# Turning band probabilities in 32x32 squares on VectorE, and band values as 32x64 tiles, in a hybrid decoder layer

## The chip, the cores and the metric

The kernel runs on one core of a Trainium2 chip. The core has five engines, each with its own instruction queue that it takes in order: TensorE (PE in the profile, with its weight loads as PEld), VectorE (DVE), ScalarE (ACT), GpSimd (POOL) and SyncE (SP), which here only issues DMAs; GpSimd issues DMAs too. Data lie in SBUF (128 partitions) and in PSUM (8 banks of 128 x 512 f32), which TensorE writes and VectorE and ScalarE read.

The metric is the device time of one execution in microseconds, lower is better. Before the change it is 1550.65 us, the median of 3 runs (1550.27 to 1556.05).

## The reference, cut to what matters

One layer over 4096 new prompt tokens (width 1024) and 64 sample tokens. After an RMS norm one projection makes the columns of three head groups: a gated short convolution, banded attention, and cross-attention into 256 memory tokens. The groups are gated, concatenated and sent through an output projection with a norm and a residual. The change concerns the banded attention of the prompt:

```python
# q (B, S, 2, 4, 64); k, v (B, S, 2, 64); blocks of 128 queries, 256 keys (previous block and own block)
qb = q.reshape(b, nb, 128, 2, 4, 64)
kk = concat([previous k block, k block]); vv = the same of v
diff = a + 128 - j                       # a: query 0..127, j: key 0..255
mask = (diff >= 0) & (diff < 128) & key exists
s = einsum('...qkgd,...skd->...kgqs', qb, kk) * 64 ** -0.5
m = max(max(where(mask, s, -inf)), sink) # one learned sink logit a head
p = exp(s - m) / (sum(exp(s - m)) + exp(sink - m))
o = einsum('...kgqs,...skd->...qkgd', p, vv)
out_b = silu(gate) * o                   # then cross-attention beside it, and the output projection
```

Every query sees exactly 128 keys: keys 0..a of its own block and keys a+1..127 of the block before. All is f32.

## The kernel before, in words

The work has two parts. The **input projection** (0 to about 950 us, products at line 359) makes all projected columns in three phases of blocks of 520 tokens and writes them to DRAM: queries and keys as pairs of a rounded value and its remainder (`qd`), V (`vd`, transposed: 128 columns of head dimension by tokens) and the gates (`md`). During its third phase `third_jobs` puts small jobs between the products: the memory keys and values, and the attention of the first 256 prompt tokens ("early").

The **attention stage** (about 950 us to the end) runs 33 blocks in order, `Block.run`: 0 to 30, 32 (the sample tokens), 31. A block is 128 output rows: two halves of 512 columns, each 24 products of 128x512 (line 1471: `y<-wo,mh` and `y<-wo,ml`, the gated mix split into a rounded part `mh` and a remainder `ml`, lines 1447 and 1450). Between these products `events_of` hangs the attention of later query groups. A group is 128 queries; a chunk is two groups (256 tokens). Names in the trace:

- `ws`: band scores, 24 products with 64 rows a tile; `xs`: 12 cross scores. ScalarE copies the own-block half into `sm` (L1140), and VectorE overwrites it with the previous-block half where the mask says so (L1141): the 128 keys that a query sees, folded into one 128x128 square a head, so `sm` is 128 x (8 heads x 128 keys).
- `band_softmax`: VectorE's maximum (`wmx`, L1147), ScalarE's eight exponentials (L1152), `wden`, `wrd` (L1153, L1154), and VectorE's product `sm` x `wrd` (L1155). `cross_softmax` does the like on `xp`, with GpSimd's scaling (L1167).
- `transposes`: eight 128x128 transposes of `sm` on TensorE (`wt`, L1194), eight of `xp` (`xt`, L1207), copies to `pt` and `xpt` by ScalarE (L1195) and VectorE or ScalarE (L1208). GpSimd's two selects take the folded square apart: `wpv` keeps the previous block's keys (L1199), `wpt` the own block's (L1201).
- `values` (`pv`): cross values in 128x64 tiles, band values in 128x64 and 64x64 tiles on V transposed by TensorE (`vtp`, L1075), into a two-bank tile; then two gates on VectorE (L1219, L1254) multiply into `mix`.

In block i: `values_and_scores` at the start of the first half makes the scores of group i+3, then the values of group i+1, then the softmax of group i+3. `transposes` at the start of the second half turns group i+2. `split` of block i+1 makes `mh` and `ml` from `mix` later in that half. At the end of each half VectorE multiplies y by the norm weights (`yn`, L1478) and ScalarE squares it (L1479); after the second half come `yst`, GpSimd's power (L1485) and the residual (`xr`, L1489).

The order on an engine is made by a scheduler from the program, except where `keep_in_program_order` holds an instruction in its place. Loads are on SP's queue (`vT`, `mix`, `xr`) and on GpSimd's (`kst`, `q`).

Of the kernel before, what the change touches and what calls it, by code (L numbers as in the profile page):

```python
# [15 lines left out]
P = 128  # L16
# [35 lines left out]
def hybrid_layer(ctx: ExitStack, tc: tile.TileContext, a: dict):  # L52
# [28 lines left out]
    vd = tc.dram_tile([P, NT], F32, name="vd")  # L81
    md = tc.dram_tile([KT, P, NT], F32, name="md")
# [711 lines left out]
    def third_jobs(b, p):  # L794
# [19 lines left out]
        if n > 13 and third["chunk"]:  # L814
            jobs.append(third["chunk"].pop(0))
        elif n > 13 and len(chunks) == 1:
            jobs.append(lambda: (chunk_load(1), chunks[1].load_values()))
# [7 lines left out]
    early = [0]  # L825

    def first_chunk():
# [5 lines left out]
        chunk.load_values()  # L833
        chunk.load_mix()
        third["chunk"] = [lambda: chunk.values(None)]
# [66 lines left out]
    def input_projection():  # L902
        for i, (ph, b, p) in enumerate(steps):
# [36 lines left out]
            if ph == 2 and b == last:  # L940
                for j in ((), (), (0, 1, 2), (3, 4, 5), (6, 7), (8, 9, 10, 11), (12, 13, 14, 15))[p]:
                    jobs.append(lambda j=j: wo_split(j))
                for j in ((), (0, 2, 4), (), (6, 8), (10, 12), (14,), ())[p]:
                    jobs.append(lambda j=j: wo_load(j))
                if p == 6:
                    jobs.append(blocks[0].split)
# [35 lines left out]
    def open_attention():  # L982
# [6 lines left out]
        ps = {tag: ctx.enter_context(tc.tile_pool(name=f"ps{tag}", bufs=1, space=bass.MemoryType.PSUM)) for tag in ("pv", "b")}  # L989
        vp = ctx.enter_context(tc.tile_pool(name="vp", bufs=5, side="right"))  # L990
# [9 lines left out]
    def psum(bank, name):  # L1000
# [3 lines left out]
        return ps["b"].tile([P, 512], F32, tag=f"b{bank}", name=name)  # L1004

    def values_psum(name):
        return ps["pv"].tile([P, 2, 512], F32, tag="pv", name=name)
# [5 lines left out]
    run_open = [False]  # L1013

    def tiled(o, w, x, **kw):

        ins = TE.matmul(o, w, x, **kw)  # L1017
        if run_open[0] and ps is not None:
            tc.keep_in_program_order(ins)
        run_open[0] = True  # L1020
# [10 lines left out]
    class Chunk:  # L1031
# [38 lines left out]
        def values(self, vt_prev, pv=None):  # L1070

            self.vts = [vt_prev]
            ts = [psum(0, f"vtp{self.c}_{i}")[:, 0:P] if pv is None else pv[:, P * i : P * i + P] for i in range(2)]
            for i in range(2):
                TE.transpose(ts[i], self.vT[:, i * P : i * P + P], ident)  # L1075
            for i in range(2):
                if self.c == 0:
                    vt = third["vt"] if i else third["work"].tile([P, P], F32, tag="v", name="vt0_0", bufs=1)
                else:
                    vt = vp.tile([P, P], F32, tag="v", name=f"vt{self.c}_{i}")  # L1080
                S.mul(vt, ts[i], 0.5)
                self.vts.append(vt)

    class Group:
# [6 lines left out]
        def open_scores(self, n):  # L1091
            b = self.b
            if n == 0:
                t = wp.tile([P, D], F32, tag="sm", name=f"sm{b}", bufs=1) if b % 2 and b > 1 else work(f"sm{b}")
                self.sm = t.rearrange("p (h k) -> p h k", h=8)
            if n == 3:
                t = wp.tile([P, D], F32, tag="p", name=f"xp{b}", bufs=1) if b % 2 and b > 1 else work(f"xp{b}")
# [45 lines left out]
        def band_softmax(self):  # L1143
# [11 lines left out]
            V.tensor_tensor(sm, sm, rd.unsqueeze(2).to_broadcast([P, n, P]), op=ALU.mult)  # L1155
# [47 lines left out]
        def cross_transposes(self, u, t):  # L1203
            t3 = t.rearrange("p (k n) -> p k n", k=2)
            for kt in range(2):
                for j in range(2):
                    TE.transpose(t3[:, kt, j * P : (j + 1) * P], self.p[:, u, j, kt * P : (kt + 1) * P], ident)  # L1207
            (S.copy if u else V.tensor_copy)(self.xpt[u], t)  # L1208
# [25 lines left out]
        def values(self):  # L1234

            c, pv = self.chunk, values_psum(f"pv{self.b}")
            self.cross_values(pv[:, 0, 256 : 256 + CT])
            o = pv[:, :, :256].rearrange("p a (h q) -> p a h q", h=4)
            step = lambda n, kvh: (c.vts[self.i + n], (self.pv, self.pt)[n][kvh].rearrange("p (h q) -> p h q", h=4))
            for n in range(2):  # L1240
                for kvh in range(2):
                    cs = slice(64 * kvh, 64 * kvh + 64)
                    v, p3 = step(n, kvh)
                    tiled(o[cs, n], v[:, cs], p3[:, :, 64 * n : 64 * n + 64], start=True, stop=False,
                          tile_position=(0, 64 * kvh))
            for n in range(2):
                for kvh in range(2):
                    cs, rs = slice(64 * kvh, 64 * kvh + 64), slice(64 - 64 * n, 128 - 64 * n)
                    v, p3 = step(n, kvh)
                    tiled(o[cs, 1 - n], v[rs, cs], p3[rs, :, 64 - 64 * n : 128 - 64 * n], start=False, stop=True,  # L1250
                          tile_position=(64 - 64 * n, 64 * kvh))
            self.cross_gate(pv[:, 0, 256 : 256 + CT])
            g = c.mix[:, 4:8, self.i * P : self.i * P + P].rearrange("p h (a q) -> p a h q", a=2)
            V.tensor_tensor(g, g, o, op=ALU.mult)  # L1254
# [3 lines left out]
    def values_and_scores(i):  # L1258

        run_open[0] = i == 0  # L1260
        g = i + 3
        if g < 2 * NCH:
            groups[g] = Group(chunks[g // 2], g % 2)
            groups[g].scores()
        if 2 <= i + 1 < 2 * NCH:
            groups.pop(i + 1).values()
        if g < 2 * NCH:
            groups[g].band_softmax()

    def transposes(i):  # L1270
        g, c = i + 2, (i + 2) // 2
        if g < 2 * NCH:
            if g % 2 == 0:
                chunks[c].values(chunks[c - 1].vts[2], psum(0, "vtp1")[:, :CT] if c == 1 else values_psum(f"vtp{c}")[:, 1, 256:])
            groups[g].transposes()
# [17 lines left out]
    def sample_mem(bh):  # L1293
# [18 lines left out]
        s = psum(3, f"sms{bh}")[:, :256]  # L1312
# [11 lines left out]
        transpose_to(pt, [(p[:, kt * P : (kt + 1) * P], P) for kt in range(2)], 3, f"smt{bh}")  # L1324
        pt = pt.rearrange("p (a c) -> p a c", a=2)
        yield
        o = values_psum(f"smo{bh}")[:, 0, :256]
# [7 lines left out]
        t = psum(3, f"smot{bh}")  # L1335
# [12 lines left out]
    def sample_window():  # L1348
# [20 lines left out]
        vn = vp.tile([P, P], F32, tag="v", name="svn")[:64]  # L1369
        transpose_to(vn, [(zs[:, 5, :], 64)], 1, "svnt")  # L1370
# [3 lines left out]
        for half in range(2):  # L1374
            s = psum(1 + half, f"sws{half}")
# [26 lines left out]
        pt, ptn = work("swpt").rearrange("p (a n) -> p a n", a=2)[:, 0], work("swptn")[:64, :512]  # L1402
        transpose_to(pt, [(sm[i][:, 0:P], P) for i in range(4)], 1, "swt0")
        transpose_to(ptn, [(sm[i][:, P:192], 64) for i in range(4)], 2, "swt1")
        pt = pt.rearrange("p (a b) -> p a b", a=4)
        yield
        o = values_psum("swo")[:, 0]
        o3 = o.rearrange("p (b c) -> p b c", b=NB)
        TE.matmul(o, vn, ptn, start=True, stop=False)
# [14 lines left out]
    class Block:  # L1424
# [28 lines left out]
        def run(self, last, events):  # L1453
# [6 lines left out]
            for p, (c0, c1) in enumerate(parts):  # L1460
                if b == 0:
                    both = values_psum("y0") if p == 0 else both
                    acc = both[:, p]
                else:
                    acc = psum((0, 5, 1)[p], f"y{b}_{p}")[:, : c1 - c0]
                j, passes = 0, 3 if m == P else 2
                for k in range(KT):
                    for fn in events.get((min(p, 1), k), ()) if p < 2 else ():
                        fn()
                    for l, r in ((0, 0), (1, 0), (0, 1)) if m == P else ((0, 0), (0, 1)):  # L1470
                        TE.matmul(acc, self.hl[l][:, k], wo[k][c0 // 512][:, r, c0 % 512 : c0 % 512 + c1 - c0], start=j == 0, stop=j == passes * KT - 1)  # L1471
# [7 lines left out]
                S.activation((psum(2, "sq") if end else acc)[:m, : c1 - c0], acc[:m], AF.Square, scale=float(D) ** -0.5, accum_out=st[:m, p : p + 1])  # L1479
# [8 lines left out]
            for cs in (slice(0, 512), slice(512, D)) if last else (slice(0, D),):  # L1488
# [6 lines left out]
    open_attention()  # L1495
    chunks[1].load_mix()
    chunk_load(2)
    chunks[2].load_values()
# [6 lines left out]
    sample = {(26, 1, 4): mem0, (27, 0, 5): mem0, (27, 1, 4): mem0, (27, 1, 6): mem0, (28, 0, 5): mem0,  # L1505
              (28, 1, 4): mem1, (29, 0, 5): mem1, (29, 1, 4): mem1, (29, 1, 6): mem1, (30, 0, 5): mem1,
              (28, 1, 5): window, (29, 0, 4): window, (29, 1, 5): window, (30, 0, 4): window}

    def events_of(i):
# [9 lines left out]
        if i % 2 == 0:  # L1519
            at(0, 1 if i else 4, chunk_load, i // 2 + 3)  # L1520
            if i // 2 + 3 < NCH:
                at(1, 3, lambda: chunks[i // 2 + 3].load_values())
            if i == 28:
                at(0, 1, lambda: chunks[15].load_mix())
        elif (i + 3) // 2 < NCH - 1:
# [123 lines left out]
```

## Time and profile before

| | |
|---|---|
| median of 3 runs | 1550.65 us |
| the profiled execution | 1549.02 us, of which the span is 1547.3 |
| granted TensorE clock in it | 0.997 of full speed |
| PE busy | 1525.7 us (99%) |
| DVE busy | 1124.6 us (73%) |
| ACT busy | 776.8 us (50%) |
| POOL busy | 335.6 us (22%) |
| DMA | 299.47 MB, q1 46.1% and q0 16.9% of 16 engines' time |

A row of a timeline gives the start in us from the span's start, the length in us, the engine, the line of the kernel, the operation, output <- inputs, and how many were merged. In brackets stands the idle time of the engine just before, and what ended it. A row of the groups gives busy time in all, the mean of one in ns, and the idle time ahead with its releasers. Lengths of matmuls overlap, since they are pipelined, so the spacing of starts tells their cost. A row of the chain of waits gives the start, the length and the engine and line that the end of the span was waiting for at that time.

### The profile page before, as it was taken

The numbers are of one execution on the slowest core, as the hardware profiler recorded it, in microseconds if no ns is written. First come the engines' busy times: TensorE is split into PE (matmuls) and PEld (weight loads), VectorE is DVE, ScalarE is ACT, GpSimd is POOL, SyncE is SP. The second block draws the span as 40 slices with busy tenths as digits, with TensorE's granted clock in tenths as the row PEclk, the third lists the DMA queues.
The fourth block names the chain that finished last, engine by engine and source line by source line (L and its number), as shares of the span: only waits on it lengthen the run. The fifth ranks groups of instructions, "written<-read, shape, count | busy, mean of one in ns | idle before, by whom it ended". The sixth has DMA issues, their size and how long they took to land.

```text
span 1547.3 us, 30906 instructions
## 1 busy us (share of the span) xinstructions
PE 1525.7 (99%) x11981; PEld 1400.8 (91%) x11981; DVE 1124.6 (73%) x1850; ACT 776.8 (50%) x1964; POOL 335.6 (22%) x522
## 2 busy tenths in 40 slices
PE   9999999999999999999999998999999999999998
PEld 9999999999999999999999997788888888888776
DVE  6779888897988777996776678566666666666654
ACT  6776566475222222344454445555555555555541
POOL 0323323220400000000000101343333434334320
PEclk9999999999999999999999999999999999999999
DMA  9979999877755333669666859744554544445432
GB/s 260 212 204 257 262 274 266 276 243 269 198 179 179 125 125 126 215 209 304 234 216 199 255 189 299 219 145 137 143 161 147 150 137 137 137 137 160 153 107 96
DMA packets 169735, 299.47 MB, mean 194 GB/s; under 512 B 29813, under 2 KB 99445, under 8 KB 169557
## 3 DMA queue, kind: packets, MB, share of 16 engines
q1 hardware_dynamic: 128069, 226.69, 46.1%
q0 software_dynamic: 40800, 69.76, 16.9%
q8 instruction: 94, 1.54, 0.4%
q10 hardware_dynamic: 720, 1.05, 0.2%
q14 instruction: 52, 0.43, 0.1%
HBM read 190.38 MB, written 108.05 MB: 193 GB/s over the span
## 4 chain that ended last, share of the span: by engine, by line
PE 88%; DVE 4%; issue 3%; DMA 2%; ACT 2%; POOL 1%; SPq 0%; DVEq 0%; POOLq 0%; ACTq 0%
PE c L359 49%; PE y L1471 24%; PE pv L1017 5%; PE ws L1017 3%; PE xt L1207 2%; PE xs L1017 2%; PE wt L1194 2%; PE mem_acc L775 1%; DMA wor<-in_w_out 1%; ACT sm L1152 1%; DMA vd<-v 1%; DVE z L366 0%; DMA wr_2A<-in_w_in 0%; DVE wo L182 0%; POOL md L163 0%
## 5 line engine op out<-in xcount | busy, mean ns | idle before, releaser
L1471 PE MATMUL y<-wo,mh 128*128 128x512 f32 (+1 forms) x1040 | 338.6, 396 | 4.6 <-ACT y L1479 3.3
L366 DVE TENSOR_TENSOR z<-c,z 128x520 f32<-128x520 f32 (+1 forms) x308 | 194.7, 645 | 96.8 <-PE c L359 95.7
L1471 PEld LDWEIGHTS y<-wo,mh 128*128 128x128 f32 x1040 | 195.5, 189 | 56.3 <-DVE sm L1141 10.8
L1471 PE MATMUL y<-wo,ml 128*128 128x512 f32 (+1 forms) x520 | 202.5, 390 | 2.7 <-DVE ml L1450 2.7
L1471 PEld LDWEIGHTS y<-wo,ml 128*128 128x128 f32 x520 | 98.5, 189 | 20.8 <-DVE ml L1450 3.0
L1163 ACT ACTIVATE xp<-xs,xnm 128x256 f32<-128x256 f32 x128 | 59.5, 471 | 115.0 <-DVE xnm L1161 101.8
L1479 ACT ACTIVATE y<-y 128x512 f32<-128x512 f32 (+1 forms) x66 | 38.2, 578 | 130.8 <-DVE yn L1478 130.8
L1167 POOL TENSOR_SCALAR xp<-xp,xrd 128x256 f32<-128x256 f32 x128 | 61.5, 491 | 181.8 <-DVE xnm L1161 111.9
L1152 ACT ACTIVATE sm<-sm,wnm 128x128 f32<-128x128 f32 x256 | 99.1, 388 | 3.0 <-DVE wnm L1148 3.0
L1199 POOL TENSOR_SCALAR_AFFINE_SELECT wpv<-wpt 128x512 f32<-128x512 f32 x62 | 62.4, 1018 | 115.5 <-ACT wpt L1195 109.8
L1153 DVE TENSOR_TENSOR wden<-wden,wes 128x8 f32<-128x8 f32 x32 | 5.3, 167 | 88.3 <-ACT sm L1152 88.3
L1478 DVE TENSOR_TENSOR yn<-y,gpost 128x512 f32<-128x512 f32 (+1 forms) x66 | 45.1, 684 | 27.1 <-PE y L1471 26.4
L1017 PEld LDWEIGHTS ws<-kst,q 64*128 64x128 f32 x768 | 48.3, 188 | 11.3 <-issue 10.5
L734 POOL MEMSET negs<- 128x1 f32 x1 | 0.1, 98 | 264.4 <-PE c L359 264.4
L1017 PE MATMUL ws<-kst,q 64*128 64x256 f32 x768 | 55.4, 290 | 0.0
L368 ACT COPY z<-c 128x520 f32<-128x520 f32 (+1 forms) x44 | 24.4, 554 | 55.5 <-PE c L359 52.9
L1201 POOL TENSOR_SCALAR_AFFINE_SELECT wpt<-wpt 128x512 f32<-128x512 f32 x64 | 40.3, 639 | 52.7 <-ACT wpt L1195 50.5
L1141 DVE COPY_PREDICATED sm<-wmask,ws 128x256 f32<-128x256 uint8 x124 | 48.0, 441 | 4.5 <-ACT sm L1140 3.2
L1485 POOL TENSOR_TENSOR yst<-yst,mhalf 128x1 f32<-128x1 f32 (+1 forms) x33 | 18.4, 557 | 151.0 <-DVE yst L1484 151.0
L1489 DVE SCALAR_TENSOR_TENSOR xr<-yn,yst,xr 128x1024 f32<-128x1024 f32 (+2 forms) x34 | 42.5, 1253 | 8.1 <-POOL yst L1485 8.1
L400 ACT CAST zh<-z 128x520 fp32r<-128x520 f32 x56 | 33.4, 624 | 29.7 <-DVE z L366 26.9
L1152 ACT ACTIVATION_READ_ACCUMULATOR sm<-sm,wnm 128x1 f32 x256 | 48.2, 188 | 0.0
(957 smaller groups left out, 5064.1 us busy)
## 6 DMA issues: line engine op xcount, KB each, us to landing
q<-qd POOLq DMA_DIRECT2D x32, 768.0 KB, 8.5
xr<-in_x_p SPq DMA_DIRECT2D x32, 512.0 KB
nat<-in_x_p SPq DMA_DIRECT2D x39, 416.0 KB
o_yp<-xr SPq DMA_DIRECT2D x31, 512.0 KB
md<-th POOLq DMA_DIRECT2D x48, 260.0 KB, 6.6
qd<-zh SPq DMA_DIRECT2D x48, 260.0 KB
qd<-z SPq DMA_DIRECT2D x48, 260.0 KB
place<-md SPq DMA_DIRECT2D x8, 1024.0 KB
```

Of the source, the lines that this page charges most:

```text
L359: TE.matmul(bank[:, :HW], l, r, start=first and i == 0, stop=last and i == 3 * KH - 1)
L366: add = lambda dst, other: V.tensor_tensor(dst, c, other, op=ALU.add)
L1017: ins = TE.matmul(o, w, x, **kw)
L1141: V.copy_predicated(to, third["wmask"], third["negs"].unsqueeze(2).to_broadcast([P, 2, P]) if self.b == 0 else s3[:, :, 0:P])
L1152: S.activation(sm[:, h, :], sm[:, h, :], AF.Exp, bias=nm[:, h : h + 1], scale=SCALE, accum_out=den[:, h : h + 1])
L1163: S.activation(p[:, i, :], s[:, i, :], AF.Exp, bias=nm[:, i : i + 1], scale=SCALE, accum_out=den[:, i : i + 1])
L1167: G.tensor_scalar(p[:, i, :], p[:, i, :], rd[:, i : i + 1], 0.5, op0=ALU.mult, op1=ALU.mult)
L1199: G.affine_select(self.pv[u].rearrange("p (h q) -> p h q", h=4), p3, pattern=[[0, 4], [-1, P]], compare_op=ALU.is_gt, fill=0.0, base=0, ch ...
L1201: G.affine_select(p3, p3, pattern=[[0, 4], [1, P]], compare_op=ALU.is_ge, fill=0.0, base=0, channel_multiplier=-1)
L1471: TE.matmul(acc, self.hl[l][:, k], wo[k][c0 // 512][:, r, c0 % 512 : c0 % 512 + c1 - c0], start=j == 0, stop=j == passes * KT - 1)
L1478: V.tensor_tensor(yn[:m, c0:c1], acc[:m], gpost[:m, c0:c1], op=ALU.mult)
L1489: V.scalar_tensor_tensor(self.xr[:m, cs], yn[:m, cs], st[:m, 3:4], self.xr[:m, cs], op0=ALU.mult, op1=ALU.add)
```

## The change

- **Turning the probabilities.** `transposes` keeps only the cross part (both copies now ScalarE's). A new `turn` takes the normalised square `sm` apart first, with two GpSimd selects of 128x1024 (`sp` for the previous block, `sm` in place for the own block), and then turns each by one VectorE transpose, which transposes every 32x32 square in its place: `t1` and `t0`, 128x1024 each.
- **Normalising.** VectorE's product `sm` x `wrd` becomes eight GpSimd scalings of 128x128, with the factor 0.5 of the gate.
- **Values.** After turns in squares, key 32k+r of query 32g+c stands in partition 32g+r. So the rows g of the array take queries 32g to 32g+31, and V must stand in all four groups of 32 partitions. Five steps (the five squares of 32 keys that a group of 32 queries touches), four row groups, two kv heads: 40 products of 32x64 tiles with 128 columns, into four PSUM banks, then four gates of 128x128.
- **V.** In the third phase, `v_load` and `v_turn` read `vd` in eight parts of 512 tokens, turn them in squares on VectorE and write them by four DMAs each to DRAM as `vn` (tokens by head dimension). `load_values` reads a chunk of it four times, once for each group of 32 partitions. TensorE's transposes of V go, except in the first chunk.
- **Order and places.** In block i: scores and softmax of group i+2 at the start of the first half; values of group i+1 at the start of the second half; `split` after its fourth step, cross transposes of group i+2 after its fifth, `turn` after its sixth. y has two banks of its own (6, 7); scores and band values share banks 0 to 3, cross scores and cross transposes banks 4 and 5. Mix and V are loaded in odd blocks. The sample stages move to other places. Transposes, the first y product and those after an event are held in program order.

```diff
+    vn = tc.dram_tile([NT - NS, P], F32, name="vn")
...
+        if n >= 15 and n % 3 == 0 and n < 39:
+            jobs.append(lambda: v_load((n - 15) // 3))
+        if n >= 17 and n % 3 == 2 and n < 41:
+            jobs.append(lambda: v_turn((n - 17) // 3))
...
+    def v_turn(k):
+        turned = temp(f"vq{k}")[:, :512]
+        V.transpose(turned, third.pop(("v", k)))
+        rows_of = vn[512 * k : 512 * k + 512, :].rearrange("(b i) d -> i b d", i=32)
+        for g in range(4):
+            ds = slice(32 * g, 32 * g + 32)
+            DMA.dma_start(rows_of[:, :, ds], turned[ds].rearrange("p (b j) -> p b j", j=32))
...
-            self.vT = self.pool().tile([P, CT], F32, tag="vT", name=f"vT{self.c}")
-            DMA.dma_start(self.vT, vd[:, self.ts])
+            self.vr = vp.tile([P, 8, P], F32, tag="vr", name=f"vr{self.c}")
+            for g in range(4):
+                DMA.dma_start(self.vr[32 * g : 32 * g + 32], vn[CT * self.c : CT * self.c + CT, :].rearrange("(b i) d -> i b d", i=32))
...
-            V.tensor_tensor(sm, sm, rd.unsqueeze(2).to_broadcast([P, n, P]), op=ALU.mult)
+            for h in range(n):
+                G.tensor_scalar(sm[:, h], sm[:, h], rd[:, h : h + 1], 0.5, op0=ALU.mult, op1=ALU.mult)
...
+        def turn(self):
+            flat = lambda t: t.rearrange("p h k -> p (h k)")
+            parts = self.sm, wp.tile([P, 8, P], F32, tag="sp", name=f"sp{self.b}", bufs=1)
+            G.affine_select(parts[1], self.sm, pattern=[[0, 8], [1, P]], compare_op=ALU.is_gt, fill=0.0, base=0, channel_multiplier=-1)
+            G.affine_select(parts[0], self.sm, pattern=[[0, 8], [-1, P]], compare_op=ALU.is_ge, fill=0.0, base=0, channel_multiplier=1)
+            self.turned = [wp.tile([P, 8, P], F32, tag=f"t{n}", name=f"t{n}_{self.b}", bufs=1) for n in range(2)]
+            for n in (1, 0):
+                tc.keep_in_program_order(V.transpose(flat(self.turned[n]), flat(parts[n])))
...
         def transposes(self):
             for u in range(2):
-                self.pt[u], self.pv[u] = (wp.tile([P, 512], F32, tag=t, name=f"w{t}{self.b}_{u}") for t in ("pt", "pv"))
-                self.band_transposes(u, psum(1 + u, f"wt{self.b}_{u}"))
-            for u in range(2):
                 self.xpt[u] = wp.tile([P, 512], F32, tag="xpt", name=f"xpt{self.b}_{u}")
-                self.cross_transposes(u, psum(3 + u, f"xt{self.b}_{u}"))
+                self.cross_transposes(u, psum(4 + u, f"xt{self.b}_{u}"))
...
-            (S.copy if u else V.tensor_copy)(self.xpt[u], t)
+            S.copy(self.xpt[u], t)
...
+            outs = [psum(g, f"wo{self.b}_{g}") for g in range(4)]
+            cross = outs[3][:, P : P + CT]
+            self.cross_values(cross)
+            for step in range(5):
+                for g in range(4):
+                    for kvh in range(2):
+                        rs, cs = slice(32 * g, 32 * g + 32), slice(64 * kvh, 64 * kvh + 64)
+                        now, k = (0, step) if step <= g else (1, step - 1)
+                        v = c.vr[rs, 4 * self.i + k, cs] if now == 0 else (last.vr[rs, 4 + k, cs] if self.i == 0 else c.vr[rs, k, cs])
+                        tiled(outs[g][cs, :P], v, self.turned[now][rs, 4 * kvh : 4 * kvh + 4, 32 * k : 32 * k + 32],
+                              start=step == 0, stop=step == 4, tile_position=(32 * g, 64 * kvh))
+            self.cross_gate(cross)
+            for g in range(4):
+                t = self.i * P + 32 * g
+                gate = c.mix[:, 4:8, t : t + 32]
+                V.tensor_tensor(gate, gate, outs[g][:, :P].rearrange("p (h q) -> p h q", h=4), op=ALU.mult)
...
-        at(0, 0 if i else 3, values_and_scores, i)
+        at(0, 0, scores, i + 2)
...
-        at(1, 0 if i else 2, transposes, i)
+        at(1, 0, values, i + 1)
         if i + 1 < len(blocks) and blocks[i + 1].b != 32:
-            at(1, 3 if i else 4, blocks[i + 1].split)
+            at(1, 4, blocks[i + 1].split)
+        at(1, 5, after_scores, i + 2, Group.transposes)
+        at(1, 6, after_scores, i + 2, Group.turn)
```

More of the change, by code (lines that the diff above doesn't have):

```diff
@@ L1068, in load_mix, with early_values @@
             DMA.dma_start(self.mix, md[:, :, self.ts].rearrange("k p n -> p k n"))
[L1070 to L1073 removed]
+        def early_values(self):
+            vT = self.pool().tile([P, CT], F32, tag="vT", name="vT0")
+            DMA.dma_start(vT, vd[:, self.ts])
+            ts = [psum(0, f"vtp{i}")[:, 0:P] for i in range(2)]
             for i in range(2):
[L1075 removed]
+                TE.transpose(ts[i], vT[:, i * P : i * P + P], ident)
+            self.vts = [None]
             for i in range(2):
[L1077 to L1081, printed above, removed]
+                vt = third["vt"] if i else third["work"].tile([P, P], F32, tag="v", name="vt0", bufs=1)
+                S.copy(vt, ts[i])
                 self.vts.append(vt)
@@ L1270, in transposes, with values, after_scores @@
[L1270 to L1275, printed above, removed]
+            groups[g].band_softmax()
+    def values(g):
+        if 2 <= g < 2 * NCH:
+            groups.pop(g).values()
+    def after_scores(g, fn):
+        if g < 2 * NCH:
+            fn(groups[g])
     def chunk_load(c):
@@ L1495, in hybrid_layer @@
     open_attention()
+    chunk_load(2)
+    for c in range(2):
+        chunks[c].load_values()
     chunks[1].load_mix()
-    chunk_load(2)
-    chunks[2].load_values()
     blocks[0].load()
```

124 lines of the change are left out of this document (50 added, 74 removed).

## The prediction

> **What bounds the kernel now.** I read the page first, then the chain that ended last, then the timelines of PE, DVE, ACT and POOL over one block of the attention stage (about 950 us to the end; one block makes 128 output rows).
>
> ```profile
> PE 1525.7 (99%) x11981; PEld 1400.8 (91%) x11981; DVE 1124.6 (73%) x1850; ACT 776.8 (50%) x1964; POOL 335.6 (22%) x522
> PE 88%; DVE 4%; issue 3%; DMA 2%; ACT 2%; POOL 1%; SPq 0%; DVEq 0%; POOLq 0%; ACTq 0%
> L366 DVE TENSOR_TENSOR z<-c,z 128x520 f32<-128x520 f32 (+1 forms) x308 | 194.7, 645 | 96.8 <-PE c L359 95.7
> ```
>
> TensorE is busy 99% of the span and is 88% of the chain. In the input projection VectorE waits for it (95.7 us ahead of L366). In the attention stage the chain shows the scores (`ws`) at the same place of every second block:
>
> ```profile
> 1137.43 1.62 PE ws L1017 x23
> 1173.46 1.62 PE ws L1017 x23
> ```
>
> Two blocks take 36.03 us, so a block takes 18.02. Its PE work, from PE's timeline:
>
> ```profile
> 1139.89 1.09 PE L1017 MATMUL pv<-xpt,mv 128*64 128x128 f32 x16
> 1140.81 0.60 PE L1017 MATMUL pv<-wpv,vt 128*64 128x256 f32 x4
> 1141.78 0.43 PE L1017 MATMUL pv<-wpv,vt 64*64 64x256 f32 x2
> 1141.79 0.43 PE L1017 MATMUL pv<-wpt,vt 64*64 64x256 f32 x2
> 1142.04 0.38 PE L1017 MATMUL pv<-wpv,vt 64*64 64x256 f32 x2
> 1142.37 0.50 PE L1471 MATMUL y<-wo,mh 128*128 128x512 f32 x1
> 1147.96 0.38 PE L1075 MATMUL vtp<-ident,vT 128*128 128x128 f32 x2
> 1148.18 1.04 PE L1194 MATMUL wt<-ident,sm 128*128 128x128 f32 x8
> 1149.05 1.04 PE L1207 MATMUL xt<-ident,xp 128*128 128x128 f32 x8
> ```
>
> **TensorE's share of the change.** Removed: the eight band transposes, 1149.05 - 1148.18 = 0.87 us a block, and the two of V, 0.22 us a chunk (0.11 a block). The band values take 1142.37 - 1140.81 = 1.56 us now. They become 40 products on eight 32x64 tiles; this trace records an f32 product as two instructions, so 80, in ten rounds of eight tiles and 128 columns. In the 64*64 part four tiles start within 0.01 us and the next round 0.26 us later for 256 columns; the cross values make eight rounds of 128 columns in 0.92 us, 0.115 each. A round then costs 0.115 to about 0.15: 1.15 to 1.5 us in all. If the 32-row tiles did not run side by side and each instruction took what one takes in the cross values (0.92/16 = 0.0575), it would be 4.6 us. I take 1.5, by the 64*64 rows, the nearest form. PE's block: 18.02 - 0.87 - 0.11 - 0.06 = 16.98 us, with ends 16.6 and 20.1. If PE stayed the bound, this would save about 1 us a block.
>
> **What the change puts in VectorE's way.** One block of the other engines, from their timelines (DVE, then ACT, then POOL):
>
> ```profile
> 1137.46 0.69 DVE L1478 TENSOR_TENSOR yn<-y,gpost 128x512 f32<-128x512 f32 x1 [0.47 <-PE y L1471]
> 1139.23 0.45 DVE L1141 COPY_PREDICATED sm<-wmask,ws 128x256 f32<-128x256 uint8 x1
> 1139.85 1.28 DVE L1489 SCALAR_TENSOR_TENSOR xr<-yn,yst,xr 128x1024 f32<-128x1024 f32 x1 [0.17 <-POOL yst L1485]
> 1143.31 1.21 DVE L1147 TENSOR_REDUCE wmx<-sm 128x8 f32<-128x1024 f32 x1
> 1144.76 0.41 DVE L1219 TENSOR_TENSOR mix<-mix,pv 128x256 f32<-128x256 f32 x1
> 1145.09 0.68 DVE L1254 TENSOR_TENSOR mix<-mix,pv 128x512 f32<-128x512 f32 x1
> 1149.33 0.20 DVE L1154 RECIPROCAL wrd<-wden 128x8 f32<-128x8 f32 x1
> 1149.57 1.22 DVE L1155 TENSOR_TENSOR sm<-sm,wrd 128x1024 f32<-128x1024 f32 x1
> 1150.71 0.68 DVE L1478 TENSOR_TENSOR yn<-y,gpost 128x512 f32<-128x512 f32 x1
> 1151.31 0.68 DVE L1208 COPY xpt<-xt 128x512 f32<-128x512 f32 x1
> 1154.12 1.23 DVE L1450 TENSOR_TENSOR ml<-mix,mh 128x1024 fp32r<-128x1024 f32 x1 [2.13 <-ACT mh L1447]
> ```
> ```profile
> 1145.79 0.39 ACT L1152 ACTIVATE sm<-sm,wnm 128x128 f32<-128x128 f32 x1
> 1148.91 0.19 ACT L1152 ACTIVATION_READ_ACCUMULATOR sm<-sm,wnm 128x1 f32 x1
> 1153.01 1.07 ACT L1447 CAST mh<-mix 128x1024 fp32r<-128x1024 f32 x1
> ```
> ```profile
> 1144.82 0.93 POOL L1167 TENSOR_SCALAR xp<-xp,xrd 128x256 f32<-128x256 f32 x2 [2.60 <-DVE xnm L1161]
> 1146.18 0.93 POOL L1167 TENSOR_SCALAR xp<-xp,xrd 128x256 f32<-128x256 f32 x2 [0.44 <-DVE wes L1149]
> 1149.96 1.33 POOL L1199 TENSOR_SCALAR_AFFINE_SELECT wpv<-wpt 128x512 f32<-128x512 f32 x1 [2.84 <-ACT wpt L1195]
> 1151.35 0.64 POOL L1201 TENSOR_SCALAR_AFFINE_SELECT wpt<-wpt 128x512 f32<-128x512 f32 x1
> masks.py:199 POOL TENSOR_SCALAR_AFFINE_SELECT ident<-ident 128x128 f32<-128x128 f32 x1 | 0.3, 284 | 0.0
> ```
>
> In the changed program, as built, VectorE's order in each block is: `yn` of the second half of block i; the four masked copies, maxima and small operations of group i+3; `yn` of the first half of block i+1; `wden` and `wrd` of group i+3; the five gates of group i+2 and `ml`; the two turns of group i+3; then `yn` of the second half of block i+1. An engine takes its queue in order, so nothing of group i+4 can start on VectorE before both turns of group i+3 are done, and these wait for GpSimd, which waits for `wrd`. The softmax of one group thus becomes a closed loop over VectorE, ScalarE and GpSimd. The old loop was shorter: from `yn` at 1137.46 through the softmax to the `yn` behind it at 1150.71, 13.25 us, well inside 18.02.
>
> The new loop, counted from that `yn`:
> - `yn`, ScalarE's square, the masked copies, the maxima and the eight exponentials up to the end of `wrd`: 1149.53 - 1137.46 = 12.07 us. The order inside is nearly the same, and its last member is the exponentials (1145.79 to 1149.10). GpSimd then starts about 0.09 us later, as `xp` at 1146.18 does behind its reciprocal: 12.16.
> - Eight scalings of 128x128 on GpSimd replace the one VectorE product of 1.22 us. The nearest row, 128x256, takes 0.465; selects grow from 0.284 us (128x128) to 0.64 (128x512), 0.93 ns an element, so half the width saves about 0.12: 0.35 each, 2.8 us. Ends: 0.23 (half of 0.465) and 0.465, 1.9 and 3.7 us. At 14.96.
> - Two selects of 128x1024: 0.64 + 512 x 0.93 ns = 1.11 us each and two gaps of 0.06: 17.3. Upper end two 128x512 each, 1.28.
> - GpSimd held up by VectorE: `wpv` at 1149.96 took 1.33 us, not 0.64, while the product at 1149.57 with two SBUF operands ran beside it, though the pair of `xp` scalings took 0.93 beside the gates, which read PSUM, as without them. `ml` has two SBUF operands. It is due inside this leg: gates from 12.1 to 13.3 (four of 128x128: 0.41 at 256 and 0.68 at 512 columns make 0.28, less 0.08 of overlap; one at 0.33; the old pair took 1.01), `mh` 1.07 and `ml` 1.23 to about 15.7. In the old row 0.69 us were lost of 0.83 beside the product; over all of `ml` that is 1.0. At 18.3. Ends: 0 and 1.25.
> - The turns: `t1` runs beside the second select; `t0` follows it. No row shows a 32x32 turn on VectorE. The nearest by size and type are the 128x1024 operations at 1.21 and 1.22 us; I take 1.22 and subtract the 0.08 by which successors overlap. The ends are 0.68 (the 128x512 copy) and 2.44, twice as long. L = 19.5 us.
>
> [...]
>
> So L = 19.5 is longer than PE's 16.98, and VectorE's loop sets the pace; PE would idle 2.5 us a block. Other edits cost nothing while this holds: the gates and `mh`/`ml` lie beside GpSimd's leg; `xpt` goes to ScalarE, which loses two `wpt` copies for it; scores and values share banks 0 to 3, but scores of group i+4 need only the gates of group i+2 (at 13.3), before PE's y needs `ml` at 15.7.
>
> V: eight loads, eight turns of 128x512 (0.68 each by the copy) and 32 stores lie in the input projection, under VectorE's waits for PE (L366). On SP's queue each store waits for its turn, and behind it stand the projection's loads; those are issued three products ahead, some 13 us. Cost 0, upper end 8 x 0.68 = 5 us. Four reloads a chunk, with one, go out two blocks early; cost 0.
>
> **Start and end.**
>
> ```profile
> 953.32 0.50 PE L1471 MATMUL y<-wo,ml 128*128 128x512 f32 x1 [2.73 <-DVE ml L1450]
> 975.36 0.69 DVE L1478 TENSOR_TENSOR yn<-y,gpost 128x512 f32<-128x512 f32 x1 [2.84 <-PE y L1471]
> 1483.44 0.69 DVE L1478 TENSOR_TENSOR yn<-y,gpost 128x512 f32<-128x512 f32 x1 [0.39 <-PE y L1471]
> 1505.50 1.09 PE L1017 MATMUL pv<-xpt,mv 128*64 128x128 f32 x16
> ```
> ```profile
> L1387 DVE COPY_PREDICATED_SCALAR ssm<-smask,negs 128x384 f32 x2 | 1.3, 656 | 3.7 <-ACT ssm L1384 3.7
> L1400 DVE TENSOR_SCALAR ssm<-ssm,swrd 128x192 f32<-128x192 f32 x4 | 1.0, 316 | 0.0
> ```
>
> Block 0 now holds no scores, and its split is issued earlier: y from about 951, 48 products at 0.233 (24 of them lie between 1142.37 and 1147.96, 5.59 us) and eight transposes later `yn` of its second half comes at 963 (end 966), not 975.4. From there 28 loops lead to block 28's `yn` (now 1483.4). Behind it, group 31: `ml` at 15.7, some 8 us of sample work that stands before the turns (the six operations of the last two rows, 2.6 us, and an estimate of 5 to 6 for some ten more, four of them exponentials), the turns 2.4: 26. Its values take 2.5. What follows took 1547.3 - 1505.5 - 2.5 = 39.3, less the 5.6 of the half block that now lies ahead: 33.7. Together 62.2 against 63.9.
>
> Span = 963 + 28 x 19.5 + 62.2 = 1571.2; with the profiled run's 1.7 us around the span (1549.02 against 1547.3), **1573 us**, against 1549.0 of that execution, itself 1.6 under the median of 1550.65. In short: time = 1027 + 28 L. Equal at L = 18.64. About 0.5% (7.75 us) is what a measurement here can tell: faster below 18.37, slower above 18.92.
>
> **Rivals.**
> 1. *Faster: GpSimd's leg is short.* If `ml` does not hold it and the scalings cost 0.3, the leg from `wrd` to the end of the selects is 4.7 us, not 6.2: L = 18.05, time 1532. It decides at a leg of about 5.05 us. Held scalings elsewhere (1.33 against 0.64) speak against; that part of `ml` may fall before the selects speaks for. The floor is PE's block: 16.98, 1502.
> 2. *The turns take 2.44 us each:* `t1` then ends behind the second select, L about 22, time 1643. No row decides this.
> 3. *PE is the bound after all,* with the values at 4.6 us: L = 20.1, time 1590. Against: four 64*64 tiles start together.
> [...]
>
> **Chances.** Loop between 18.9 and 20.5, the forecast: 0.49, slower. Loop 18.4 to 18.9: 0.10, same. Rival 1: 0.24, faster. Rival 2: 0.09, rival 3: 0.08, both slower. So slower 0.66. The forecast's own range is 1556 to 1601. The range over all leaves out the far ends of rivals 1 and 2: 1526 to 1622.
>
> **What would show it.** Right: in the changed kernel VectorE's turn waits for GpSimd's select, the chain of waits in this stage runs through exponentials, scalings, selects and turns, PE idles about 2.5 us a block, and blocks are 19.5 us apart. Wrong: PE stays near 99% and blocks are 17 us apart (rival 1), or a turn row shows over 2 us, or the values' group spans over 3 us. A clock row below 1.00 in PE's new gaps would add time that no term here holds.

## The result and the profile after

The changed kernel takes 1602.79 us (median of 4 runs, 1601.2 to 1605.24), the kernel before 1550.46 (median of 4): ratio 1.033, 95% interval 1.0303 to 1.0358. It is slower by 52 us, where the prediction had it slower by 24. The profiled execution has a span of 1600.1 us against 1547.3.

The page, its busy times and the chain that ended last by engine:

```profile
PE 1517.6 (95%) x13631; PEld 1396.0 (87%) x13631; DVE 1145.8 (72%) x1944; ACT 760.7 (48%) x1906; POOL 428.4 (27%) x718
...
DVE 10%; POOL 10%; ACT 10%; PE 5%; issue 3%; DMA 2%; SPq 0%; ACTq 0%; POOLq 0%; DVEq 0%
```

TensorE was busy 8 us less than before. The two chains are not of one length: of TensorE's 88% before, 49% are products of the input projection (L359 on the page), and the chain of the changed kernel is followed back to 958.9 us only. So outside the input projection TensorE fell from 39% of the span to 5%. In its place stand VectorE, GpSimd and ScalarE with 10% each: the loop of the forecast. One turn of it in the middle of the stage, from VectorE's timeline and then GpSimd's:

```profile
1154.67 0.65 DVE L1491 TENSOR_TENSOR yn<-y,gpost 128x512 f32<-128x512 f32 x1
...
1166.53 0.20 DVE L1165 RECIPROCAL wrd<-wden 128x8 f32<-128x8 f32 x1
...
1168.93 1.23 DVE L1464 TENSOR_TENSOR ml<-mix,mh 128x1024 fp32r<-128x1024 f32 x1 [1.11 <-ACT mh L1461]
1171.94 1.25 DVE L1205 STREAM_TRANSPOSE t<-sp 128x1024 f32<-128x1024 f32 x1 [1.78 <-POOL sp L1201]
1173.11 1.24 DVE L1205 STREAM_TRANSPOSE t<-sm 128x1024 f32<-128x1024 f32 x1
1174.27 0.65 DVE L1491 TENSOR_TENSOR yn<-y,gpost 128x512 f32<-128x512 f32 x1
```
```profile
1166.90 3.84 POOL L1168 TENSOR_SCALAR sm<-sm,wrd 128x128 f32<-128x128 f32 x8 [2.55 <-ACT y L1492]
1170.81 1.09 POOL L1201 TENSOR_SCALAR_AFFINE_SELECT sp<-sm 128x1024 f32<-128x1024 f32 x1
1171.97 1.09 POOL L1202 TENSOR_SCALAR_AFFINE_SELECT sm<-sm 128x1024 f32<-128x1024 f32 x1
```

From `yn` to `yn` are 1174.27 - 1154.67 = 19.60 us, and the first turn stands 1.78 us waiting for the first select. TensorE shows the price, in its own timeline:

```profile
1159.39 1.77 PE L1032 MATMUL wo<-xpt,mv 128*64 128x128 f32 x16 [2.42 <-DVE sm L1152]
1161.09 2.27 PE L1032 MATMUL wo<-t,vr 32*64 32x128 f32 x80
```

It idles 2.42 us ahead of the values; over the stage there are 24 such waits, 46.5 us in all, 1.9 us each. So the block is as forecast (19.5), and 26 of the 29 us that the forecast lacks lie outside the 26 steady blocks. The `yn` of the second half of blocks 1 and 27 in the kernel before, then of blocks 0, 1, 27 and 28 in the changed one (VectorE's timeline of each):

```profile
993.08 0.69 DVE L1478 TENSOR_TENSOR yn<-y,gpost 128x512 f32<-128x512 f32 x1 [0.30 <-PE y L1471]
...
1465.05 0.69 DVE L1478 TENSOR_TENSOR yn<-y,gpost 128x512 f32<-128x512 f32 x1 [2.29 <-PE y L1471]
```
```profile
970.26 0.65 DVE L1491 TENSOR_TENSOR yn<-y,gpost 128x512 f32<-128x512 f32 x1
...
997.84 0.69 DVE L1491 TENSOR_TENSOR yn<-y,gpost 128x512 f32<-128x512 f32 x1 [2.24 <-PE y L1482]
...
1507.60 0.65 DVE L1491 TENSOR_TENSOR yn<-y,gpost 128x512 f32<-128x512 f32 x1
...
1532.75 0.69 DVE L1491 TENSOR_TENSOR yn<-y,gpost 128x512 f32<-128x512 f32 x1 [0.83 <-PE y L1482]
```

| stretch | before | forecast | after | after less forecast |
|---|---|---|---|---|
| to `yn` of block 0 | 975.36 | 963 | 970.26 | +7.3 |
| block 0 to 1 | 17.72 | 19.5 | 27.58 | +8.1 |
| block 1 to 27 (26 blocks) | 471.97 | 507 | 509.76 | +2.8 |
| block 27 to 28 | 18.39 | 19.5 | 25.15 | +5.65 |
| block 28 to the end | 63.86 | 62.2 | 67.35 | +5.15 |
| span | 1547.3 | 1571.2 | 1600.1 | +28.9 |

Against the kernel before, 37.8 of the 52.8 us are the 26 blocks of the loop. What stretched block 1 stands in the chain (start, length, what) and in the groups of instructions:

```profile
958.93 8.79 DMA qd<-z
969.89 1.58 SPq L1067
971.52 14.88 DMA vr<-vn
986.64 3.47 PE wo L1032 x78
```
```profile
L1032 PE MATMUL wo<-t,vr 32*64 32x128 f32 x2400 | 50.8, 309 | 11.9 <-DMA vr<-vn 11.9
```

The reloads of V (L1067) come out of SP's queue at 967.7, behind the last stores of `z`, and the last of the eight lands at 986.4; TensorE stood 11.9 us for them. Block 28 has another one, in TensorE's timeline:

```profile
1519.52 0.69 PE L1351 MATMUL smot<-ident,sq 128*128 128x128 f32 x2 [4.24 <-ACT sq L1346]
```

A transpose of the sample attention waits for a copy that ScalarE has queued behind the exponentials of a group, and everything behind it on TensorE waits too.

### The profile page after: what moved, and what is told of

It reads as the page before. It is cut to its first block, busy times and chain, and to the rows that moved or that the text cites. A ratio compares the mean times of both kernels' runs of the same rounds, so it can differ in the third digit from the quotient of the medians.

```text
span 1600.1 us, 34589 instructions
## 1 busy us (share of the span) xinstructions
PE 1517.6 (95%) x13631; PEld 1396.0 (87%) x13631; DVE 1145.8 (72%) x1944; ACT 760.7 (48%) x1906; POOL 428.4 (27%) x718
## 5 line engine op out<-in xcount | busy, mean ns | idle before, releaser
L1482 PE MATMUL y<-wo,mh 128*128 128x512 f32 (+1 forms) x1040 | 347.9, 401 | 0.0
L1168 POOL TENSOR_SCALAR sm<-sm,wrd 128x128 f32<-128x128 f32 x256 | 123.4, 503 | 170.1 <-DVE wrd L1165 88.7
L1032 PE MATMUL wo<-xpt,mv 128*64 128x128 f32 x480 | 38.4, 310 | 46.5 <-DVE sm L1152 46.5
L1032 PEld LDWEIGHTS wo<-xpt,mv 128*64 128x64 f32 x480 | 30.0, 154 | 59.1 <-DVE sm L1152 56.6
L1205 DVE STREAM_TRANSPOSE t<-sp 128x1024 f32<-128x1024 f32 x30 | 37.3, 1245 | 44.6 <-POOL sp L1201 44.6
L1032 PE MATMUL wo<-t,vr 32*64 32x128 f32 x2400 | 50.8, 309 | 11.9 <-DMA vr<-vn 11.9
L1032 PEld LDWEIGHTS wo<-t,vr 32*64 32x64 f32 x2400 | 42.8, 150 | 18.5 <-issue 18.1
```

Source lines behind the costliest of these rows:

```text
L1032: in_order_here(TE.matmul(o, w, x, **kw))
L1168: G.tensor_scalar(sm[:, h], sm[:, h], rd[:, h : h + 1], 0.5, op0=ALU.mult, op1=ALU.mult)
L1205: tc.keep_in_program_order(V.transpose(flat(self.turned[n]), flat(parts[n])))
L1482: ins = TE.matmul(acc, self.hl[l][:, k], wo[k][c0 // 512][:, r, c0 % 512 : c0 % 512 + c1 - c0], start=j == 0, stop=j == passes * KT - 1)
```

## Experiments

Theory A: the loop over VectorE, ScalarE and GpSimd sets the block; the missing 29 us are waits at the start and in the sample stage. Rival B: the block is set by the values' wait for banks 0 to 3. Rival C: the eight scalings are what is paid. The kernel before took 1553 to 1556 us (medians) beside these runs, so ratios to it are compared; the changed kernel's is 1.033.

**The loop opened.** The selects stay, the turns go behind the maxima of the next group, the values three steps of the product later (`between` is a new argument of `band_softmax`; `select` is the first half of the old `turn`, `turn` its second half):

```diff
             for h in range(n):
                 S.activation(sm[:, h, :], sm[:, h, :], AF.Exp, bias=nm[:, h : h + 1], scale=SCALE, accum_out=den[:, h : h + 1])
+            if between:
+                between()
             V.tensor_tensor(den, den, es, op=ALU.add)
...
-            groups[g].band_softmax()
+            groups[g].band_softmax(groups[g - 1].turn)
...
-        at(1, 0, values, i + 1)
+        at(1, 3, values, i + 1)
-        at(1, 6, after_scores, i + 2, Group.turn)
+        at(1, 6, after_scores, i + 2, Group.select)
```

> The two turns of a group move behind the masked copies and maxima of the next group in VectorE's order, and the band values three steps of the product later on TensorE, so that they find the turned squares; nothing else moves. Theory A (the loop over VectorE, ScalarE and GpSimd sets 19.6 us a block): the loop is open, TensorE's own work sets the pace, 17.0 us a block, 26 blocks save 68 us, about 1535 us. Rival B (the pace comes from the values waiting for banks 0 to 3, or from GpSimd's amount of work): the block stays above 19 us, and the run above 1590 us.

Measured: 1537.2 us, ratio 0.988 (0.9847 to 0.9913), 1.2% under the kernel before. From its page the chain (back to 961.4 us only, so that its 34% are nearly all of it), and one block of VectorE and of GpSimd:

```profile
PE 34%; DMA 2%; DVE 1%; ACT 0%; SPq 0%; issue 0%; DVEq 0%; POOLq 0%; POOL 0%; ACTq 0%
```
```profile
1201.85 0.69 DVE L1497 TENSOR_TENSOR yn<-y,gpost 128x512 f32<-128x512 f32 x1 [0.84 <-PE y L1488]
...
1209.40 1.24 DVE L1209 STREAM_TRANSPOSE t<-sp 128x1024 f32<-128x1024 f32 x1
...
1210.60 1.22 DVE L1209 STREAM_TRANSPOSE t<-sm 128x1024 f32<-128x1024 f32 x1
...
1216.53 1.48 DVE L1470 TENSOR_TENSOR ml<-mix,mh 128x1024 fp32r<-128x1024 f32 x1 [1.11 <-ACT mh L1467]
1218.83 0.69 DVE L1497 TENSOR_TENSOR yn<-y,gpost 128x512 f32<-128x512 f32 x1 [0.82 <-PE y L1488]
```
```profile
1214.12 2.81 POOL L1170 TENSOR_SCALAR sm<-sm,wrd 128x128 f32<-128x128 f32 x8 [2.40 <-ACT y L1498]
1217.01 1.95 POOL L1201 TENSOR_SCALAR_AFFINE_SELECT sp<-sm 128x1024 f32<-128x1024 f32 x1
1219.02 1.09 POOL L1202 TENSOR_SCALAR_AFFINE_SELECT sm<-sm 128x1024 f32<-128x1024 f32 x1
```

The block is 1218.83 - 1201.85 = 16.98 us, the work that the prediction counted for TensorE (that it agrees to the digit is luck, since that sum had ends of 16.6 and 20.1); `yn` waits for TensorE again, the turns for nothing. Theory A holds. GpSimd's rows tell a second thing: `ml` now falls beside the first select, and it is the select that takes 1.95 us instead of 1.09, while the scalings take 2.81 instead of 3.84. The hold-up follows `ml`, and here `ml` itself takes 1.48 instead of 1.23.

**Half of it.** Only the values later (of the diff above the lines with `values` alone):

> Only the place of the band values on TensorE moves: three steps of the product later, so that they no longer wait 2.4 us for the masked copies to free banks 0 to 3. Rival B (this wait sets the pace): block 17.2 us, ratio to before about 0.99. Theory A (the loop over VectorE, ScalarE and GpSimd): TensorE idles the same 2.4 us at another place, block 19.6 us, ratio 1.033.

Measured: ratio 1.027 (1.0226 to 1.0315). Two `xr`, one block apart, and the values' row:

```profile
1191.92 1.28 DVE L1502 SCALAR_TENSOR_TENSOR xr<-yn,yst,xr 128x1024 f32<-128x1024 f32 x1 [0.69 <-POOL yst L1498]
...
1211.17 1.28 DVE L1502 SCALAR_TENSOR_TENSOR xr<-yn,yst,xr 128x1024 f32<-128x1024 f32 x1 [0.67 <-POOL yst L1498]
```
```profile
1213.20 1.09 PE L1032 MATMUL wo<-xpt,mv 128*64 128x128 f32 x16
```

The values no longer wait, and the block is 19.25 us, not 17.2: rival B falls. The 0.35 us that it did gain are VectorE's own: two of the masked copies now stand ahead of `xr`, and from `yn` to `wrd` are 11.53 us instead of 11.86.

And only the turns later (the other lines alone):

> Only the turns move behind the next group's maxima, the values stay at their old place on TensorE. By the trace of the open loop the second turn ends 10.0 us after yn, and at their old place the values are due 7.9 us after it: TensorE waits 2.05 us a block for the turns, 16.98 + 2.05 = 19.0 us a block, ratio to before 1.023. If the wait for the banks is what counts: as the open loop, 0.99.

Measured: ratio 1.0069 (1.004 to 1.0099), 18.05 us a block. TensorE's rows:

```profile
1210.78 1.09 PE L1032 MATMUL wo<-xpt,mv 128*64 128x128 f32 x16
1212.87 1.43 PE L1032 MATMUL wo<-t,vr 32*64 32x128 f32 x80 [1.00 <-DVE t L1209]
```

TensorE waits 1.00 us for the turns, not 2.05: the expectation forgot that the cross values, which need no turn, come first and take 1 us. 16.98 + 1.00 is 17.98. Opening the loop is the larger part of the gain, and the values' place 1.07 us more.

**GpSimd and `ml`.** The same subtraction done twice:

```diff
-            V.tensor_tensor(lo, src, f(hi), op=ALU.subtract)
+            for _ in range(2):
+                V.tensor_tensor(lo, src, f(hi), op=ALU.subtract)
```

> The subtraction that makes ml (two operands in SBUF, 1.23 us) is done twice over, with the same result; VectorE has 1.8 us of idle time behind it, and TensorE does not need ml until about 1 us after the second. Theory A (the product with two SBUF operands holds GpSimd up, which is why eight scalings take 3.84 us and not 2.80): GpSimd's leg grows by another 0.5 (only the scalings are held) to 1.1 us (the selects too), block 20.1 to 20.7 us, 1616 to 1632 us. Rival (the scalings simply take 0.48 us each, nothing holds them): block 19.6 us, 1603 us.

Measured: 1633.87 us (two runs, 1628.19 and 1639.54), ratio 1.0501 (1.0408 to 1.0594), just above the expected range. The profiled run, the longer one, was 7.5 us late already in the input projection, where nothing differs yet (its first `mem_acc` product at 720.4 against 712.9), so the block is what counts. From its chain:

```profile
1009.44 1.29 DVE xr L1503
...
1016.59 2.12 ACT sm L1163 x11
1019.32 4.80 POOL sm L1168 x8
...
1030.00 1.28 DVE xr L1503
```

The block is 20.56 us, 0.96 longer, and the scalings take 4.80 us, 0.96 longer: one more `ml`, one more microsecond of GpSimd. In the changed kernel itself the scalings that no `ml` meets take 2.80 (block 1, where TensorE waits for V, and a late block):

```profile
981.16 2.80 POOL L1168 TENSOR_SCALAR sm<-sm,wrd 128x128 f32<-128x128 f32 x8 [2.55 <-ACT y L1492]
...
1519.82 2.80 POOL L1168 TENSOR_SCALAR sm<-sm,wrd 128x128 f32<-128x128 f32 x8 [2.55 <-DVE wrd L1165]
```

So in these traces the two hold each other up: `ml`, 1.23 us elsewhere, costs GpSimd 0.86 (beside a select) to 1.04 us (beside the scalings), and beside the select it takes 1.48 us itself.

**The normalising back on VectorE.** One part of the change undone:

```diff
-            for h in range(n):
-                G.tensor_scalar(sm[:, h], sm[:, h], rd[:, h : h + 1], 0.5, op0=ALU.mult, op1=ALU.mult)
+            V.scalar_tensor_tensor(sm, sm, 0.5, rd.unsqueeze(2).to_broadcast([P, n, P]), op0=ALU.mult, op1=ALU.mult)
```

> One part of the change undone: the normalising is again one product on VectorE (with the factor 0.5 in it), the rest as changed. Rival C (the eight scalings are what is paid): the block falls by 3.84 less 1.22 us, to TensorE's 17.0, about 1535 us. Theory A with VectorE's order counted out: product to 13.3 us after yn, gates to 14.6, mh to 15.8, ml to 17.0, and only then the two turns, to 19.4, while the selects are done at 15.7: ml takes the place of the selects as the last wait, block 19.3 us, about 1595 us.

Measured: 1588.05 us, ratio 1.0207 (1.017 to 1.0244), 18.99 us a block.

```profile
1200.53 1.23 DVE L1166 SCALAR_TENSOR_TENSOR sm<-sm,wrd 128x1024 f32<-128x1024 f32 x1
...
1203.99 1.23 DVE L1462 TENSOR_TENSOR ml<-place,mh 128x1024 fp32r<-128x1024 f32 x1 [1.11 <-ACT mh L1459]
1205.14 1.23 DVE L1203 STREAM_TRANSPOSE t<-sp 128x1024 f32<-128x1024 f32 x1
```

That is near theory A's 19.3 and far from rival C's 17.0. Taking 2.6 us out of the loop gave 0.6: the turns now stand right behind `ml` in VectorE's queue, with nothing waited for. Rival C falls; the queue's order is the cost, and GpSimd's scalings are only one of two legs of nearly the same length.

**The start.** V of the first two chunks reloaded among the jobs of the input projection's last steps (for this the tiles of V have other places in SBUF):

```diff
+        if n in (43, 44):
+            jobs.append(chunks[n - 43].load_values)
...
-    for c in range(2):
-        chunks[c].load_values()
```

> Only the reloads of V for the first two chunks move: they are issued some 30 us before the attention stage (of chunk 0 only the upper half, which alone is read), where the changed kernel issued them from 967.7 us on. Theory A (the start is late because TensorE waits 11.9 us for the replicated V): that wait goes, block 0 to block 1 shrinks from 27.6 to about 19.6 us, the block time after it stays 19.6, and the run takes about 1595 us. Rival (the DMA engines are full there, so another transfer, mix or the keys, ends as late): unchanged, 1603 us.

Measured: 1608.38 us, ratio 1.0337 (1.0284 to 1.0391): no gain. From its chain and VectorE's timeline:

```profile
971.25 15.94 DMA gpost<-in_gpost
```
```profile
987.31 1.29 DVE L1494 TENSOR_TENSOR yn<-y,gpost 128x512 f32<-128x512 f32 x2 [11.47 <-DMA gpost<-in_gpost]
```

The wait for V was gone, block 0 to 1 took 15.7 us (`xr` to `xr`), but the scheduler had put `gpost` behind the stores of `z`, and block 0 waited for that instead. With `gpost` held in front of them (`gpost_load` is its load, kept in program order):

```diff
-                    jobs.insert(0, blocks[0].split)
+                    jobs[:0] = [blocks[0].split, gpost_load]
```

> As the run with V reloaded early, and gpost is issued ahead of the last stores of z, as it was in the changed kernel (in that run it had slipped behind them and TensorE waited 16.8 us). If the start of the stage is held by which load comes last in the queue of loads: block 1 ends its yn some 8 to 13 us earlier than in the changed kernel, 1.6% of the time before less at most, ratio to before about 1.026. If the DMA engines are full whatever the order: the ratio stays at 1.033.

Measured: 1597.53 us, ratio 1.028 (1.0247 to 1.0314). The last product of the input projection in the changed kernel (block 1's `yn` is above), then here, from TensorE's timeline, and block 1's `yn` here, from VectorE's:

```profile
952.33 0.28 PE L360 MATMUL c<-hi_7T,w_2A 128*128 128x260 f32 x1
```
```profile
954.45 0.28 PE L360 MATMUL c<-hi_7T,w_2A 128*128 128x260 f32 x1
```
```profile
991.96 0.65 DVE L1501 TENSOR_TENSOR yn<-y,gpost 128x512 f32<-128x512 f32 x1
```

45.5 us from the one to the other in the changed kernel, 37.5 here: 8.0 us, the lower end of what was expected. The ratio alone hardly tells the two kernels apart (their intervals touch); the rows do.

**The projection's share of V.** The kernel before, with the loads, turns and stores of V added and nothing reading them:

> The kernel before, with only the V work of the input projection added: eight loads, eight turns of 128x512 on VectorE and 32 stores of V by rows, whose result nothing reads (the attention stage is that of before). The prediction put this at 0, with 5 us as the upper end. If 0: ratio 1.000. If the turns and stores delay the projection: up to 1.003. If the input projection is where the unexplained time of the changed kernel comes from: 1.005 or more.

Measured: 1554.4 us over 12 runs against 1553.02, ratio 1.0015 (0.9997 to 1.0033): by the runs, 0 to 5 us, as bounded. The traces are sharper. On TensorE, from the first `mem_acc` product of the third phase to the last product of the projection, are 948.51 - 713.97 = 234.5 us in the kernel before and 953.33 - 718.90 = 234.4 here, so V's work shows no cost there. In the changed kernel the same stretch takes 952.33 - 712.93 = 239.4 us. Of these 4.9 us more, 3.4 are five waits for the scalings that are now GpSimd's, in the attention of the first groups; one of them, from TensorE's timeline of the changed kernel:

```profile
799.21 1.02 PE L1214 MATMUL wt<-ident,sm 128*128 128x128 f32 x3 [1.07 <-POOL sm L1168]
```

**The sample stage.** The changed kernel with three stages moved:

```diff
-    ... (27, 1, 6): mem0, (28, 0, 4): mem0, (28, 0, 6): mem0,
+    ... (28, 0, 2): mem0, (28, 0, 5): mem0, (28, 1, 4): mem0,
```

> The changed kernel, with three stages of the sample attention's first half issued later on TensorE and nothing else. If the 4.2 us that TensorE stands waiting for ScalarE's copy there (which is queued behind the exponentials of a group) is what makes block 28 last 25.2 us instead of 19.6: block 28 at 19.6 to 21 us, 4 to 6 us less in all, ratio 1.029. If block 28 is long because of the work itself: ratio 1.033.

Measured: 1604.34 us, ratio 1.0327 (1.0298 to 1.0355). The whole run can't tell 5 us; the rows of blocks 27 and 28 can:

```profile
1509.42 0.65 DVE L1491 TENSOR_TENSOR yn<-y,gpost 128x512 f32<-128x512 f32 x1
...
1529.80 0.69 DVE L1491 TENSOR_TENSOR yn<-y,gpost 128x512 f32<-128x512 f32 x1
```

20.4 us instead of 25.15: the wait, 4.24 us before and at most 0.63 for that copy here, was the reason for 4.8 of the 5.65 us that this block is over the forecast.

**All together.** The open loop, V and `gpost` early, the sample stages moved:

> The open loop (turns and values moved), with V and gpost early, and the sample attention's transposes and products of the first half issued later on TensorE (in the run of the open loop they waited 2.05 us for VectorE and 4.06 us for ScalarE). Each part as measured alone: 16.98 us a block; 8 to 13 us less at the start; up to 6 us less near the end; ratio to before 0.988 less 0.009 to 0.012, about 0.978. If the start is bound by the DMA engines: 0.985.

Measured: 1522.95 us, ratio 0.9805 (0.9775 to 0.9834), between the two expectations. TensorE has no wait of more than 2.2 us left in the attention stage, and the block is 16.98 us. With its queues in another order, the changed kernel's way of forming the band products is faster than the kernel before: by 1.2% with the turns and values moved alone, by 1.95% with the rest. What the early `gpost` and the later sample stages would give the kernel before was not tried.

## Why the prediction was right and wrong

Right: the sign, the mechanism and the size of the block. L was forecast at 19.5 and is 19.60. By its terms: `yn` to the start of GpSimd's scalings 12.16, measured 1166.90 - 1154.67 = 12.23; scalings 2.8, measured 2.80 where free; held up by `ml` 1.0, measured 1.04 (on the scalings, not on the selects behind them); a select 1.11, measured 1.09; a turn 1.22, measured 1.24 and 1.25. TensorE's block without the loop 16.98, measured 16.98 in the run of the open loop. Its idle time was forecast at 2.5 us a block; its 24 waits are 1.9 us on average, and some of the rest went into slower products (last section). The turn takes what other 128x1024 operations of VectorE take in the changed kernel: 1.21 us for `wmx`, 1.23 for `ml`, 1.28 for `xr`. Rival 1 (a short leg on GpSimd), rival 2 (turns of 2.44 us) and rival 3 (TensorE the bound) all fell: rival 1 would have needed `ml` to hold nothing up, and the 80 products, 4.6 us in rival 3, take 1.43 us in the open loop.

Wrong: the size, 24 us for 52. The step that failed is the terms outside the loop, 1027 us in the formula "time = 1027 + 28 L": with the measured L of 19.60 they come to 1602.79 - 548.8 = 1054. In the prediction's words:
- "Four reloads a chunk, with one, go out two blocks early; cost 0." True of the chunks from the third on. The first two chunks have no earlier block: their eight loads stand behind the stores of `z` in SP's queue, and block 0 to 1 took 8.1 us more than forecast; with V and `gpost` loaded earlier, 8.0 us came back. The prediction followed SP's queue past the new stores, but not past the new loads at the stage's first block.
- "Block 0 now holds no scores ... `yn` of its second half comes at 963." TensorE begins the block at 952.45, 1.5 us after the 951 of the forecast; the waits for GpSimd's scalings in the input projection (3.4 us) had no term. Its first `yn` starts at 964.15, 5.5 us after VectorE is free for it; what held it was not tested. Behind it in VectorE's queue stand `ml` of the next block and both turns of group 2: 970.26, 7.3 us late. That is the loop's own order, which the prediction used for every block but this one.
- "From there 28 loops lead to block 28's `yn`." The sample attention's first half lies in that stretch; block 27 to 28 is 5.65 us over the loop, and the run with three of its stages later took 4.8 of them away with one wait of TensorE. The kernel before showed one such long block too (21.2 us, ending with block 27), which the forecast passed over.
- The tail, 62.2, was 67.35. The turns of group 31 ended 25.4 us behind block 28's `yn` (26 forecast), but TensorE had products of the sample attention and of y ahead of the values in its queue and began the values at 1561.87, 29.1 us behind it; from the end of the values to the end are 35.8 us, where 33.7 were forecast. This was not tested by itself.

The forecast's own range, 1556 to 1601, ended just below the result; of these four terms the start had an end of 966, V one of 5 us for the input projection, and the two others had none.

## What to carry to other kernels

Moving an operation to an engine with idle time is priced by what stands behind it in the queues, not by its duration: here two turns of 1.24 us, put ahead of the next group's work, closed a loop of 19.6 us around a TensorE that needed 17.0; behind that work, and with the values moved to match, they let the block fall to 16.98. When a forecast multiplies one steady block, give the first block, the last, and any that carries extra work a line of their own, with each new load's place in its queue. When a wait is taken away, look for the one that was just behind it: with V early, `gpost` took its place and nothing was gained.

## What was not expected of the hardware

GpSimd loses 0.86 to 1.04 us to one VectorE subtraction of 1.23 us with both operands in SBUF: scalings 2.80 to 3.84, select 1.09 to 1.95, and with two subtractions scalings 4.80. The prediction had this from a single row; that it would be so exact was not expected. VectorE loses too: 1.48 us instead of 1.23 for the `ml` beside the select in the open loop. In the run with `gpost` early one `ml` in block 0 took 2.60 us; why was not shown.

Some of TensorE's products took longer behind its idle times. The same 80 products of the values took 1.43 us in most blocks, behind an idle time of about 2.4 as well, but 1.96 to 2.38 us in eight others, 2.27 in the one shown above behind the same 2.42, and 3.47 behind the 11.9 us wait for V. The stretches of time by engine show the granted clock of that one block and of the 10 us of the long wait (columns: stretch, length, PE, PEld, DVE, ACT, POOL busy, PE clock, DMA share, GB/s):

```profile
1157.04:1176.62 19.58, 17.23 (x183) 14.52 (x184) 12.20 (x28) 9.59 (x37) 8.50 (x16) 0.91 0.34 109
```
```profile
980.00:990.00 10.00, 3.36 (x80) 2.85 (x80) 0.60 (x4) 1.16 (x6) 4.99 (x10) 0.50 1.19 311
```

The clock was 0.91 and 0.50 there, and 1.00 in the blocks on either side of the first. The block shown is no longer for it (19.58 us), since TensorE was not the bound there. In block 1 the chain runs through these very products, so 3.47 - 1.43 = 2.0 us of its 27.58 go with the slower clock; a clock row below 1.00 was the prediction's sign of time that no term of it holds.
